# Token sums spread over the projection's last blocks, later statistics, and the first gates whole ahead of w_a

## The chip, the core and the metric

The kernel runs on one core of a Trainium2 chip. Its time is the device time of one execution in microseconds (us); lower is better. Five engines work side by side, each through its own queue in order: TensorE (PE) multiplies, VectorE (DVE), ScalarE (ACT) and GpSimd (POOL) do elementwise work, and SyncE (SP) issues most DMA transfers. An instruction at the head of a queue that waits for another engine holds up all that stands behind it in that queue.

## The reference, cut to what matters

One layer of a hybrid decoder, 1024 tokens and 16 meta tokens, width 1024, all in float32. Three branches are mixed through sigmoid gates, projected back, and followed by a SwiGLU MLP.

```python
xn = rms_norm(h, norm1_g)
p = xn @ w_in
(u_pool, q, c_lat, q_idx, k_idx, w_idx, cb, cc, cu, g_raw) = split_columns(p)
y_a = pool_mixer(u_pool, pool_w, pool_scale) @ w_a
attn = dsa_attention(q, q_idx, w_idx, rms_norm(c_lat, kv_norm_g), k_idx)   # top-k selection, then attention
y_b = attn @ w_b
y_c = short_conv_mixer(cb, cc, cu, conv_w) @ w_c
g = sigmoid(g_raw + b_gate).reshape(B, L, 3, 1024)
m = g[:, :, 0] * y_a + g[:, :, 1] * y_b + g[:, :, 2] * y_c
h = h + m @ w_o
hn = rms_norm(h, norm2_g)
gate, up = split(hn @ w_gate_up, 2)
h = h + (silu(gate) * up) @ w_down
return rms_norm(h, final_g)[:, 16:]
```

## The kernel before, in words

**Arithmetic.** A float32 factor is held as a high part (`whi`, `xh`, a cast on ACT) and a low part (`wlo`, `xl`, a subtraction on DVE or POOL, L288 in `sub_lo`). A product of two factors is three matmuls: high by high (L261), high by low (L262), low by high (L263). Tokens stand in two chunks of 512 columns, and outputs in tiles of 128 rows, so nearly every matmul is 128x128 by 512 columns. A large projection is cut into two by two blocks and computed with seven products instead of eight. For that, sums of the token blocks ("token sums", the keys T1 to T4) and sums of the weight blocks (the `sw` tiles, on POOL) are made first, and each is split into high and low parts before PE can use it. A product has four blocks of 128 along its inner dimension, so 12 matmuls; `CHAINED` is the order of the seven products of a job or of an MLP tile `f`. Four of the seven end in a result that is read from a PSUM bank as `c` by an ACT copy and later added to (DVE) as the other products come.

**Order.** The order of the work is written out by hand. `gemm` issues the matmuls and calls at its k-th step what a table `at` hangs there. `later` holds what consumes the product before it. `ahead` and `make_ahead` issue the making of weight factors a fixed number of products before PE needs them. `settle` issues low parts that were put off in `behind`. Since the queues run in order, a step that is called earlier in the program stands earlier in every queue that it uses. The indexer's top-k search (L726, L771, L772 on DVE, L790 to L796 on ACT) fills gaps from a background list, at a pace set by `pace_until`.

**The gates** (`gates`, `plan_gates`, from L1000). The first of these jobs is a plain product with two weights ("in" units). Before w_a, each weight is multiplied with chunk 1 only; after w_a, the same two weights come again (the "again" units, loaded and split a second time) and are multiplied with chunk 0, 24 matmuls each. Then come the chained products n=0, 1, 2 and so on, whose factors are made `n + 5` ahead. The token sum T4 of the input (L1253, three DVE operations for each of four blocks, then a cast L1268 and a low part) is spread by `PLAIN` and `SCHED` over these products.

**The output projection** (`out_proj`) runs blocks (o, ch) for output tile o and chunk ch. Blocks 0 to 4 take both chunks in turn, then 5, 6, 7 take chunk 0, then chunk 1. A block ends in an add of the residual (L1706, DVE), a scaling (L1696), a square (L1715, ACT) and an accumulation (L1719, POOL). Between its matmuls the token sums of the MLP are made: `first` (L1740, splits of the scaled tokens), `t1`, `t2`, `t3`. The norm's statistics are small matmuls (L1648) of the accumulated squares: `stat(0)` for chunk 0, `stat1` for chunk 1; `ratio` (L1663) spreads a statistic over the partitions.

**The MLP** (`mlp`) begins with f=0. The table `entry` hangs what is left of the token sums and statistics on its products. `pair_sums` (L1862 to L1865) are the four POOL sums of the weights of a tile f; they wait for its weights to be loaded (`raw`). For w_down, blocks of its weights are loaded by `load_w` (L2007) at slots counted from its first product, activations come back by `load_x` (L2014), and `split_x` (L2022) splits them.

Of the kernel before, what the change touches and what calls it, by code (L numbers as in the profile page):

```python
# [16 lines left out]
P = 128  # L17
# [37 lines left out]
SCHED = {0: (("T4b", 0), ("T4", 1)), 1: (("T4b", 1), ("T4", 2)), 2: (("T4b", 2), ("T4", 3)), 3: (("T4b", 3),),  # L55
         4: (("lo", 0),)}
# [22 lines left out]
def unit_plan():  # L79
# [22 lines left out]
    units.append(("again", cols[0], KT))  # L102
    units.append(("again", cols[0] + 4 * P, KT))
# [17 lines left out]
class Trunk:  # L121
    SLACK = 1500.0

    def __init__(self, tc, a):
# [806 lines left out]
    def branch_a(self):  # L931
# [72 lines left out]
        for j in range(2):  # L1004
            w = wg if j == 0 else self.get()
            xs = self.xn_real(1)
            if j == 0:
                pool_split(0)
                pool_product(1)
            ps = self.gemm(w, xs, 512)  # L1010
            if j:
                pool_product(0)
            t = self.t(self.xp, [P, 512], tag="b")
            self.gate(kind, o + 4 * j, t, ps)
            nc.sync.dma_start(self.sgd[kind, o + 4 * j, 1], t)
# [23 lines left out]
    def plan_gates(self):  # L1039
# [6 lines left out]
        n_op = 0  # L1046
# [12 lines left out]
        def plan(j):  # L1059
# [12 lines left out]

            def make(i):
                if not src:
                    start()
                factor(src[i], LO[i])
                if i == 0:
                    total(2, src["u", 0], src["u", 1], ALU.add)
                    total(4, src[2], src[0], ALU.subtract)
# [21 lines left out]
    def gates(self):  # L1101
# [70 lines left out]
        w = [self.get(), self.get(ahead=False)]  # L1172
        self.lo_engine = "pool"
        self.plan_gates()
        for a in range(2):
            self.make_ahead(PA[a])
            for name, k in PLAIN[a]:
                T[name](k)
            ps = self.gemm(w[a], self.xn_real(0), 512)
            self.later.append(lambda ps=ps, a=a: res(0, a, 0, copied(ps)))  # L1180
            flush_stores()
# [7 lines left out]
        for n, (j, i) in enumerate(self.order):  # L1189
            self.make_ahead(n + 5)  # L1190
# [476 lines left out]
    def out_proj(self):  # L1667
# [6 lines left out]
        self.opp = self.pool("op", 1)  # L1674
        tp = self.otp = self.pool("ot", 1)
# [24 lines left out]
        def block(w, o, ch, at=None):  # L1700
# [9 lines left out]
            if o == 0:  # L1710
                acc[ch] = self.t(tp, [P, 512], tag=f"acc{ch}")
# [9 lines left out]
        def first_stat(ch):  # L1721
            first_st[ch] = self.row_rstd([acc[ch], last[ch]], tp, scale=1.0 / 512, tag="rsp")
# [39 lines left out]
        def c(f, *a):  # L1762
# [8 lines left out]
              (4, 0): {1: c(bcast, 0), 3: c(first_stat, 1), 5: c(first, 0), 7: c(first, 1)},  # L1771
              (4, 1): {0: c(bcast, 1), 1: c(first, 2), 3: c(first, 3), 5: c(t1, 0), 7: c(t1, 1)}}
# [566 lines left out]
```

## Time and profile before

| | |
|---|---|
| median of 3 runs | 1720.79 us (1720.04 to 1721.91) |
| the profiled execution | 1719.1 us, of which its span is 1717.3 us |
| granted TensorE clock, mean over the span | 0.990 |
| PE busy | 1660.8 us, 97% of the span, 8008 matmuls |
| DVE, ACT, POOL busy | 74%, 45%, 42% |
| PE's share of the chain that ended last | 65% |

Every time below is counted from the start of the span. In a view of the timeline the columns are: start, length, engine, line, operation, output and input tiles, size, how many; and in brackets how long the engine was idle before it and what it waited for. A clock of 1.00 in a stretch is 2.4 GHz, 0.50 is 1.2 GHz.

### The profile page before, as it was taken

The numbers are of one execution on the slowest core, as the hardware profiler recorded it, in microseconds if no ns is written. First come the engines' busy times: TensorE is split into PE (matmuls) and PEld (weight loads), VectorE is DVE, ScalarE is ACT, GpSimd is POOL, SyncE is SP. The second block draws the span as 40 slices with busy tenths as digits, with TensorE's granted clock in tenths as the row PEclk, the third lists the DMA queues.
The fourth block names the chain that finished last, engine by engine and source line by source line (L and its number), as shares of the span: only waits on it lengthen the run. The fifth ranks groups of instructions, "written<-read, shape, count | busy, mean of one in ns | idle before, by whom it ended". The sixth has DMA issues, their size and how long they took to land.

```text
span 1717.3 us, 22774 instructions
## 1 busy us (share of the span) xinstructions
PE 1660.8 (97%) x8008; PEld 1383.6 (81%) x8008; DVE 1279.2 (74%) x2156; ACT 780.1 (45%) x1463; POOL 719.7 (42%) x537
## 2 busy tenths in 40 slices
PE   8989999998999999999999998999999999999998
PEld 7778878886888887888878876788888888778887
DVE  6999997578888853688787367666666666799787
ACT  5566227455544435776632233433333333444443
POOL 2412324415555766121075113555445554546043
PEclk9999999999999999999999998999999999999999
DMA  4111123132333343410077431323232333663433
GB/s 155 46 37 35 40 86 105 68 124 88 127 115 99 98 129 90 132 50 13 17 268 255 135 123 49 104 92 105 98 105 92 111 115 138 226 233 125 160 97 117
DMA packets 94227, 189.09 MB, mean 110 GB/s; under 512 B 9808, under 2 KB 23120, under 8 KB 94112
## 3 DMA queue, kind: packets, MB, share of 16 engines
q1 hardware_dynamic: 91008, 182.56, 31.7%
q10 hardware_dynamic: 2992, 4.75, 0.8%
q8 instruction: 63, 1.03, 0.3%
q0 software_dynamic: 112, 0.33, 0.1%
q14 instruction: 52, 0.43, 0.1%
HBM read 133.86 MB, written 53.74 MB: 109 GB/s over the span
## 4 chain that ended last, share of the span: by engine, by line
PE 65%; DVE 5%; DMA 2%; ACT 1%; issue 1%; SPq 0%; POOL 0%; ACTq 0%; DVEq 0%; POOLq 0%
PE ps L261 19%; PE ps L263 19%; PE ps L262 19%; PE ps L1452 2%; PE ps L1428 1%; PE ps L1429 1%; PE ps L1427 1%; PE ps L1476 1%; PE ps L1477 1%; PE ps L1478 1%; PE ps L1648 1%; DVE wlo L232 0%; DMA s<-ga 0%; DVE y L1696 0%; DVE B21l L288 0%
## 5 line engine op out<-in xcount | busy, mean ns | idle before, releaser
L261 PE MATMUL ps<-xh,whi 128*128 128x512 f32 (+1 forms) x492 | 174.2, 354 | 4.3 <-DVE u L869 2.4
L263 PE MATMUL ps<-xh,wlo 128*128 128x512 f32 (+1 forms) x492 | 173.6, 353 | 1.1 <-DVE wlo L232 1.1
L262 PE MATMUL ps<-xl,whi 128*128 128x512 f32 (+1 forms) x492 | 173.4, 352 | 0.6 <-POOL xl L288 0.4
L261 PE MATMUL ps<-h,whi 128*128 128x512 f32 x348 | 137.8, 396 | 3.8 <-ACT whi L226 2.4
L263 PE MATMUL ps<-h,wlo 128*128 128x512 f32 x352 | 138.3, 393 | 1.5 <-DVE wlo L232 1.5
L262 PE MATMUL ps<-l,whi 128*128 128x512 f32 x288 | 113.5, 394 | 1.3 <-DVE l L288 1.2
L261 PEld LDWEIGHTS ps<-xh,whi 128*128 128x128 f32 x492 | 93.1, 189 | 17.4 <-DVE u L869 2.8
L263 PEld LDWEIGHTS ps<-xh,wlo 128*128 128x128 f32 x492 | 93.2, 189 | 14.8 <-DVE wlo L232 1.9
L262 PEld LDWEIGHTS ps<-xl,whi 128*128 128x128 f32 x492 | 93.2, 190 | 13.3 <-POOL xl L288 1.2
L1862 POOL TENSOR_TENSOR l<-raw 128x512 f32<-128x512 f32 x21 | 30.8, 1468 | 153.9 <-DMA raw<-in_wts_dram 142.7
L232 POOL TENSOR_TENSOR wlo<-raw,whi 128x1024 fp32r<-128x1024 f32 x21 | 51.7, 2462 | 99.5 <-ACT whi L226 99.5
L726 DVE TENSOR_SCALAR_CACHE_REDUCE B<-sc,s 128x912 bf16<-128x912 f32 (+2 forms) x93 | 89.0, 958 | 0.1
L1917 ACT ACTIVATE c<-c 128x512 f32<-128x512 f32 x44 | 27.8, 632 | 125.4 <-DVE c L1954 125.4
L261 PEld LDWEIGHTS ps<-h,whi 128*128 128x128 f32 x348 | 65.7, 189 | 18.7 <-ACT whi L226 3.3
L263 PEld LDWEIGHTS ps<-h,wlo 128*128 128x128 f32 x352 | 66.5, 189 | 16.7 <-DVE wlo L232 2.4
L1954 DVE TENSOR_TENSOR c<-c,r 128x512 f32<-128x512 f32 x88 | 60.5, 688 | 17.6 <-ACT c L1917 15.4
L1913 ACT COPY c<-ps 128x512 f32<-128x512 f32 x66 | 38.7, 587 | 66.5 <-PE ps L263 63.8
L262 PEld LDWEIGHTS ps<-l,whi 128*128 128x128 f32 x288 | 54.5, 189 | 14.7 <-DVE l L288 2.8
L1908 DVE TENSOR_TENSOR c<-ps,c 128x512 f32<-128x512 f32 x66 | 45.3, 687 | 27.2 <-PE ps L263 27.1
L2026 POOL TENSOR_TENSOR raw<-raw,h 128x512 f32<-128x512 f32 (+1 forms) x12 | 18.6, 1547 | 102.6 <-DVE whi L288 48.6
L288 DVE TENSOR_TENSOR op<-raw,op 128x512 fp32r<-128x512 f32 (+1 forms) x43 | 34.3, 798 | 34.8 <-ACT op L1803 17.8
L1138 ACT COPY c<-ps 128x512 f32<-128x512 f32 x52 | 30.4, 585 | 63.9 <-PE ps L263 63.9
(556 smaller groups left out, 5465.3 us busy)
## 6 DMA issues: line engine op xcount, KB each, us to landing
raw<-in_wts_dram SPq DMA_DIRECT2D x120, 512.0 KB, 3.3
B<-y SPq DMA_DIRECT2D x33, 256.0 KB, 2.0
y<-b SPq DMA_DIRECT2D x32, 256.0 KB, 2.2
s<-y SPq DMA_DIRECT2D x32, 256.0 KB, 4.9
h<-in_wts_dram SPq DMA_DIRECT2D x24, 256.0 KB, 5.3
T<-h SPq DMA_DIRECT2D x22, 256.0 KB, 2.1
T<-y SPq DMA_DIRECT2D x22, 256.0 KB, 2.0
ga<-c SPq DMA_DIRECT2D x16, 256.0 KB, 3.6
```

What stands on the lines that cost most here:

```text
L232: e.tensor_tensor(l[:, c], r[:, c], h[:, c].bitcast(F32), op=ALU.subtract)
L261: nc.tensor.matmul(ps[:, c0:c0 + n], wh, xh, start=(start and k == 0), stop=False, **kw)
L262: nc.tensor.matmul(ps[:, c0:c0 + n], wh, xl, start=False, stop=False, **kw)
L263: nc.tensor.matmul(ps[:, c0:c0 + n], wl, xh, start=False, stop=(stop and k == last), **kw)
L288: getattr(self.nc, eng).tensor_tensor(lo, x, hi.bitcast(F32), op=ALU.subtract)
L726: nc.vector.tensor_scalar(junk2[:, :nk_of(i)], self.sc[i], value, None, op0=ALU.is_ge, op1=ALU.add, accum_out=at(cs, i))
L1138: nc.scalar.copy(t, ps)
L1452: nc.tensor.transpose(p3[:rows, h, :], d["S"][h][:, col:col + rows], self.ident)
L1862: e.tensor_tensor(s1, u[:, :512], u[:, 512:], op=ALU.add)
L1908: nc.vector.tensor_tensor(t, ps, t, op=ALU.add)
L1913: nc.scalar.copy(t, ps)
L1954: nc.vector.tensor_tensor(t, x, R[r], op=ALU.mult)
```

## The change

Three places are rewritten.

*The first gates.* The two plain weights are multiplied with both chunks ahead of w_a, and the "again" units are gone. w_a is followed at once by the chained products. Their factors 0 and 1 are made in w_a's last group, the first weight sums on POOL only after it, and `LEAD` makes factors 3 and more products ahead only as PE goes on (3 at n=0, 7 at n=3). The four blocks of T4 are hung on n=1, 2 and 3.

*The end of the output projection and the MLP's entry.* The steps `first`, `t1`, `t2`, `t3` move to later blocks, `stat(0)` from block (5, 1) to (6, 1), `ratio(0)` from block (6, 1) to the MLP's product n=1, `stat1` from n=0 to n=2, `ratio(1)` from n=1 to n=3. Squares and sums of chunk 1 lie in a new pool that is released after n=2. The four low and high parts of T4 are settled at n=4 instead of n=3.

*The start of w_down.* The first blocks "11" of w_down go to the homes of the `sw` tiles instead of the two `raw` buffers, and loads stand at other slots. The c tiles of the MLP get 6 buffers instead of 8.

```diff
-SCHED = {0: (("T4b", 0), ("T4", 1)), 1: (("T4b", 1), ("T4", 2)), ...
+SCHED = {1: (("T4", 0), ("T4", 1)), 2: (("T4b", 0), ("T4", 2)), ...
+LEAD = {0: 3, 1: 4, 2: 5, 3: 7}
...
-    units.append(("again", cols[0], KT))
-    units.append(("again", cols[0] + 4 * P, KT))
...
             w = wg if j == 0 else self.get()
-            xs = self.xn_real(1)
-            ...
-            ps = self.gemm(w, xs, 512)
+            for ch in (1, 0):
+                ...
+                ps = self.gemm(w, self.xn_real(ch), 512)
+                ...
+                self.gate(kind, o + 4 * j, t, ps)
...
         for op in range(4):
             self.act_on = 0 < op < 3
-            w = self.get()
+            w = self.get(ahead=op < 3)
+            if op == 3:
+                self.lo_engine = "pool"
+                self.plan_gates()
             for j in range(2):
                 for ch in range(2):
+                    if op == 3:
+                        self.make_ahead(2 if j and ch else j)
...
+            def first_sums():
+                total(2, src["u", 0], src["u", 1], ALU.add)
+                total(4, src[2], src[0], ALU.subtract)
...
-        w = [self.get(), self.get(ahead=False)]
-        self.lo_engine = "pool"
-        self.plan_gates()
-        for a in range(2):
-            self.make_ahead(PA[a])
-            ...
-            ps = self.gemm(w[a], self.xn_real(0), 512)
-            ...
+        self.first_sums()
...
-            self.make_ahead(n + 5)
+            self.make_ahead(LEAD.get(n, n + 5))
...
-                sq = self.t(tp, [P, 512], tag="sq", bufs=2)
+                sq = self.t(self.o2p, [P, 512], tag="sq", bufs=2)
...
-        block(w5, 5, 1, {1: c(first, 7), 3: c(stat, 0), 4: c(t2, 0), 6: c(t3, 0)})
+        block(w5, 5, 1, {1: c(first, 6), 2: c(self.ahead, 1), 4: c(t1, 3), 6: c(first, 7)})
...
-        return self.t(cs, [P, 512], tag="c", bufs=8)
+        return self.t(cs, [P, 512], tag="c", bufs=6)
...
-                if o % 2 == 0:
-                    pair = self.t(self.wp, [P, 1024], tag="raw", bufs=2)
-                    W[g, "11", o], W[g, "11", o + 1] = pair[:, :n], pair[:, 512:512 + n]
-                t = W[g, "11", o]
+                pool, tag = self.home("sw", (1, 0, 3, 2)[o])
+                t = W[g, "11", o] = self.t(pool, [P, 512], tag=tag)[:, :n]
...
-            when(-7 + o // 2, load_w, 0, "11", o)
+            when(-7 + 2 * (o // 2), load_w, 0, "11", o)
...
-        entry = {0: {0: lambda: [self.t2(3), self.settle()], 3: stat1},
-                 1: {1: lambda: self.ratio(1), ...
-                 ... 2: {0: each(t4, 0, 1), 2: lambda: [each(t4, 2, 3)(), self.settle()]}}
+        entry = {0: {0: lambda: [self.t2(3), self.settle()], 2: lambda: self.t3(2)},
+                 ...
+                 4: {0: stat1, 1: each(b22, 0, 1), 3: each(b22, 2, 3)},
+                 2: {0: lambda: self.ratio(1), 1: each(t4, 0, 1)},
+                 5: {0: lambda: [each(t4, 2, 3)(), self.settle()]}}
+        hold = {0: 3, 1: 4}
...
-                ahead(n_done - 1 + AHEAD)
+                ahead(hold.get(n_done - 1, n_done - 1 + AHEAD))
...
-                if cs is None:
-                    ahead(6)
+                if n_done == 1:
                     self.otp.release()
                     cs = self.pool("cs", 1, side="right")
+                if n_done == 3:
+                    ahead(6)
+                    self.o2p.release()
```

The first place, ACT's queue where w_a ends and the chained products begin. Before, the first chained weight sums (`whi`, `wlo` from `sw`), the copies of the two plain products and two T4 casts:

```order
L1053 CAST whi_3885<-sw_3850 128x512
L1053 CAST wlo_3888<-sw_3848 128x512
L1138 COPY c_3906<-ps_3857 128x512
L1230 ACTIVATE c_3906<-c_3906,cols_115 128x512
L1053 CAST whi_3930<-sw_3855 128x512
L1268 CAST T4h_772_3933<-c_3895 128x512
L1138 COPY c_3947<-ps_3899 128x512
L1230 ACTIVATE c_3947<-c_3947,cols_115 128x512
L1053 CAST wlo_3957<-sw_3891 128x512
L1268 CAST T4h_778_3960<-c_3936 128x512
L1138 COPY c_3975<-ps_3940 128x512
```

And now, from the cast of the first weight sum on; `ps_3904` is the bank that n=0, 2, 4 and 6 use in turn:

```order
L1054 CAST whi_3899<-sw_3897 128x512
L1054 CAST wlo_3917<-sw_3895 128x512
L1152 COPY c_3939<-ps_3904 128x512
L1054 CAST op_3947<-sw_3902 128x512
L1273 CAST T4h_771_3950<-c_3924 128x512
L1054 CAST op_3973<-sw_3920 128x512
L1054 CAST whi_3976<-raw_3689 128x512
L1273 CAST T4h_777_3981<-c_3928 128x512
L1235 ACTIVATE c_3939<-c_3939,cols_115 128x512
L1152 COPY c_3997<-ps_3904 128x512
```

Both copies of the bank now stand behind steps of the chained products: the first behind the two weight casts, the second behind two T4 casts and an activation of `c_3939`.

DVE's queue of the changed kernel from the low part of that first weight sum to the add whose result `c_3939` the activation reads:

```order
L284 TENSOR_TENSOR whi_3899<-sw_3897,whi_3899 128x512
L1258 TENSOR_TENSOR c_3924<-xh_5_84,s_3487 128x512
L1258 TENSOR_TENSOR c_3924<-c_3924,xl_21_100 128x512
L1258 TENSOR_TENSOR c_3924<-c_3924,s_3488 128x512
L1258 TENSOR_TENSOR c_3928<-xh_6_85,s_3489 128x512
L1258 TENSOR_TENSOR c_3928<-c_3928,xl_22_101 128x512
L1258 TENSOR_TENSOR c_3928<-c_3928,s_3490 128x512
L284 TENSOR_TENSOR op_3947<-sw_3902,op_3947 128x512
L1258 TENSOR_TENSOR c_3953<-xh_7_86,s_3491 128x512
L1258 TENSOR_TENSOR c_3953<-c_3953,xl_23_102 128x512
L1258 TENSOR_TENSOR c_3953<-c_3953,s_3492 128x512
L1147 TENSOR_TENSOR c_3939<-ps_3932,c_3939 128x512
```

Nine T4 operations and two low parts stand ahead of the add. In the kernel before, T4's first block stood beside the plain products and the first add of a chained product stood behind all twelve:

```order
L288 TENSOR_TENSOR T4l_773_3934<-c_3895,T4h_772_3933 128x512
L1253 TENSOR_TENSOR c_3964<-xh_7_86,s_3435 128x512
L1253 TENSOR_TENSOR c_3964<-c_3964,xl_23_102 128x512
L1253 TENSOR_TENSOR c_3964<-c_3964,s_3436 128x512
L288 TENSOR_TENSOR op_3984<-raw_3843,op_3984 128x512
L288 TENSOR_TENSOR T4l_779_3961<-c_3936,T4h_778_3960 128x512
L1253 TENSOR_TENSOR c_3993<-xh_8_87,s_3437 128x512
L1253 TENSOR_TENSOR c_3993<-c_3993,xl_24_103 128x512
L1253 TENSOR_TENSOR c_3993<-c_3993,s_3438 128x512
```

So the sums of T4 moved from beside the plain products to between the chained ones.

The second place, POOL's queue at the MLP's entry (f=0, before the weights of f=1 are used). Before, from the last accumulation of squares; `y` outputs of L288 are low parts of T4, `l` outputs of L1862 to L1865 the weight sums of f=1:

```order
L1719 TENSOR_TENSOR acc_1818_9261<-acc_1818_9261,sq_9896 128x512
L288 TENSOR_TENSOR l_2043_10114<-y_1920_9826,h_2040_10102 128x512
L288 TENSOR_TENSOR l_2050_10141<-y_1947_9943,h_2044_10116 128x512
L288 TENSOR_TENSOR y_2055_10157<-y_1893_9678,h_2051_10143 128x512
L288 TENSOR_TENSOR y_2058_10163<-y_1909_9762,h_2056_10159 128x512
L1862 TENSOR_TENSOR l_2060_10174<-raw_10136 128x512
L1863 TENSOR_TENSOR l_2061_10175<-l_2060_10174,raw_9872 128x512
L1864 TENSOR_TENSOR l_2062_10176<-raw_9872,l_2061_10175 128x512
L1865 TENSOR_TENSOR l_2063_10177<-raw_9872,raw_10136 128x512
```

And now:

```order
L1725 TENSOR_TENSOR acc_1812_9250<-acc_1812_9250,sq_9869 128x512
L284 TENSOR_TENSOR l_2036_10105<-y_1914_9798,h_2033_10089 128x512
L284 TENSOR_TENSOR l_2044_10134<-y_1937_9918,h_2037_10107 128x512
L1868 TENSOR_TENSOR l_2049_10154<-raw_10121 128x512
L1869 TENSOR_TENSOR l_2050_10155<-l_2049_10154,raw_9857 128x512
L1870 TENSOR_TENSOR l_2051_10156<-raw_9857,l_2050_10155 128x512
L1871 TENSOR_TENSOR l_2052_10157<-raw_9857,raw_10121 128x512
L284 TENSOR_TENSOR y_2054_10164<-y_1877_9639,h_2045_10136 128x512
L284 TENSOR_TENSOR y_2057_10170<-y_1898_9739,h_2055_10166 128x512
```

The two low parts of T4 changed places with the four weight sums of f=1.

The third place, SP's queue of transfers at the start of w_down. Before (x2 marks two transfers of one form in a row):

```order
L2007 DMA raw_13162<-in_wts_dram 128x512 x2
L2007 DMA raw_13183<-in_wts_dram 128x512 x2
L2014 DMA B11l_2523_13187<-B_1949_9949 128x512
L2014 DMA B11l_2525_13190<-B_1950_9950 128x512
L1925 DMA B_1959_9959<-y_2519_13172 128x512
L2014 DMA B11l_2530_13212<-B_1951_9951 128x512
L2014 DMA B11l_2532_13215<-B_1952_9952 128x512
```

And now:

```order
L2011 DMA l_2511_13152<-in_wts_dram 128x512
L2011 DMA l_2512_13154<-in_wts_dram 128x512
L2018 DMA B11l_2517_13175<-B_1939_9924 128x512
L2018 DMA B11l_2519_13178<-B_1940_9925 128x512
L1931 DMA B_1949_9934<-y_2514_13163 128x512
L2011 DMA l_2523_13199<-in_wts_dram 128x512
L2011 DMA l_2524_13201<-in_wts_dram 128x512
L2018 DMA B11l_2526_13204<-B_1941_9926 128x512
L2018 DMA B11l_2528_13207<-B_1942_9927 128x512
```

Two activations (`B11l`) are now asked for between the first and the second pair of weights, and the weights go to `l` tiles instead of `raw` buffers.

## Rows read from the trace of the kernel before

**Rows 1.** The page: the span, and busy time of each engine.

```profile
span 1717.3 us, 22774 instructions
PE 1660.8 (97%) x8008; PEld 1383.6 (81%) x8008; DVE 1279.2 (74%) x2156; ACT 780.1 (45%) x1463; POOL 719.7 (42%) x537
```

**Rows 2.** Timeline of PE: w_a's end, the waiting chained product, n=6 and the next.

```profile
386.81 0.39 PE L261 MATMUL ps<-xh,whi 128*128 128x512 f32 x1
...
410.46 0.79 PE L261 MATMUL ps<-s,whi 128*128 128x512 f32 x1 [5.59 <-ACT c L1138]
...
424.90 0.40 PE L261 MATMUL ps<-T4h,op 128*128 128x512 f32 x1
...
427.64 0.40 PE L261 MATMUL ps<-xh,op 128*128 128x512 f32 x1
```

**Rows 3.** Window: busy PE, PEld, DVE, ACT, POOL; PE's clock, DMA share, GB/s.

```profile
410.00:415.00 5.00, 4.54 (x11) 3.57 (x12) 4.90 (x7) 2.07 (x4) 1.70 (x1) 0.50 0.50 174
```

**Rows 4.** Timeline of ACT at the first gates.

```profile
390.62 1.07 ACT L921 COPY b<-ps 128x512 f32<-128x512 f32 x2
...
409.31 0.62 ACT L1268 CAST T4h<-c 128x512 fp32r<-128x512 f32 x1 [2.32 <-DVE c L1253]
409.83 0.58 ACT L1138 COPY c<-ps 128x512 f32<-128x512 f32 x1
```

**Rows 5.** Timeline of DVE at the first gates.

```profile
403.37 1.84 DVE L288 TENSOR_TENSOR whi<-sw,whi 128x512 fp32r<-128x512 f32 x1 [1.15 <-ACT whi L1053]
...
409.80 0.68 DVE L1253 TENSOR_TENSOR c<-xh,s 128x512 f32<-128x512 f32 x1
```

**Rows 6.** The page's DMA issues: count, size, median time to landing.

```profile
raw<-in_wts_dram SPq DMA_DIRECT2D x120, 512.0 KB, 3.3
...
y<-b SPq DMA_DIRECT2D x32, 256.0 KB, 2.2
```

**Rows 7.** Timeline of PE: start of block (5, 0), and of f=1.

```profile
1009.38 0.39 PE L261 MATMUL ps<-h,op 128*128 128x512 f32 x1
...
1084.93 0.39 PE L261 MATMUL ps<-B11h,wlo 128*128 128x512 f32 x1
```

**Rows 8.** PE's waits from 1000 to 1100: line, for what, us, times, longest.

```profile
PE ps L1648 <- ACT sq L1715: 4.8, 1, 4.8
PE ps L1648 <- POOL acc L1719: 2.8, 1, 2.8
PE ps L261 <- ACT whi L226: 2.4, 2, 2.0
PE ps L263 <- DVE wlo L232: 1.5, 2, 0.8
```

**Rows 9.** Timeline of DVE at the end of the projection.

```profile
1049.77 0.68 DVE L1706 TENSOR_TENSOR xt<-ps,xt 128x512 f32<-128x512 f32 x1
...
1060.22 0.68 DVE L1706 TENSOR_TENSOR xt<-ps,xt 128x512 f32<-128x512 f32 x1
```

**Rows 10.** Timeline of POOL from the projection's end to f=1.

```profile
1049.37 1.63 POOL L1864 TENSOR_TENSOR sw<-raw,sw 128x512 f32<-128x512 f32 x1
...
1076.01 3.16 POOL L288 TENSOR_TENSOR y<-y,h 128x512 fp32r<-128x512 f32 x2 [2.46 <-ACT h L1826]
1079.32 1.54 POOL L1862 TENSOR_TENSOR l<-raw 128x512 f32<-128x512 f32 x1 [0.15 <-DMA raw<-in_wts_dram]
...
1083.89 1.74 POOL L1865 TENSOR_TENSOR l<-raw,raw 128x512 f32<-128x512 f32 x1
```

**Rows 11.** PE's waits from 1470 to 1530, at the start of w_down.

```profile
PE ps L261 <- ACT c L1913: 2.1, 1, 2.1
PE ps L262 <- DVE B21l L288: 1.6, 1, 1.6
```

**Rows 12.** Timeline of SP's queue at the start of w_down.

```profile
1465.44 10.16 SPq L2007 DMA_DIRECT2D raw<-in_wts_dram  x4
```

**Rows 13.** Timeline of DVE at the start of w_down.

```profile
1481.10 0.70 DVE L288 TENSOR_TENSOR B11l<-B11l,B11h 128x512 fp32r<-128x512 f32 x1 [5.18 <-ACT B11h L2022]
```

More of the change, by code (lines that the diff above doesn't have):

```diff
@@ L1005, in branch_a @@
             w = wg if j == 0 else self.get()
-            xs = self.xn_real(1)
-            if j == 0:
-                pool_split(0)
-                pool_product(1)
-            ps = self.gemm(w, xs, 512)
[L1011 to L1015, printed above, removed]
+            for ch in (1, 0):
+                if j == 0 and ch:
+                    pool_split(0)
+                    pool_product(1)
+                ps = self.gemm(w, self.xn_real(ch), 512)
+                if j and ch:
+                    pool_product(0)
+                t = self.t(self.xp, [P, 512], tag="b")
+                self.gate(kind, o + 4 * j, t, ps)
+                nc.sync.dma_start(self.sgd[kind, o + 4 * j, ch], t)
         self.token_sums()
@@ L1075, in make @@
                     start()
-                factor(src[i], LO[i])
+                factor(src[i], LO[i] if j or i != 4 else "vector")
                 if i == 0:
-                    total(2, src["u", 0], src["u", 1], ALU.add)
-                    total(4, src[2], src[0], ALU.subtract)
+                    if j:
+                        first_sums()
+                    else:
+                        self.first_sums = first_sums
+                elif i == 1 and not j:
+                    self.first_sum5 = sum5
+                elif i == 4 and not j:
+                    self.first_sum5()
                 elif i == 1:
@@ L1721, in first_stat @@
         def first_stat(ch):
-            first_st[ch] = self.row_rstd([acc[ch], last[ch]], tp, scale=1.0 / 512, tag="rsp")
+            first_st[ch] = self.row_rstd([acc[ch], last[ch]], self.o2p, scale=1.0 / 512, tag="rsp")
             nc.gpsimd.tensor_tensor(acc[ch], acc[ch], last[ch], op=ALU.add)
@@ L1770, in out_proj @@
         at = {(3, 1): {4: c(first_stat, 0)},
-              (4, 0): {1: c(bcast, 0), 3: c(first_stat, 1), 5: c(first, 0), 7: c(first, 1)},
-              (4, 1): {0: c(bcast, 1), 1: c(first, 2), 3: c(first, 3), 5: c(t1, 0), 7: c(t1, 1)}}
+              (4, 0): {1: c(bcast, 0), 3: c(first_stat, 1)},
+              (4, 1): {0: c(bcast, 1), 1: c(first, 0), 4: c(first, 1)}}
         for o in range(5):
@@ L1777, in out_proj @@
         w5 = self.get()
-        block(w5, 5, 0, {2: c(t1, 2), 4: c(t1, 3), 6: c(first, 4)})
+        block(w5, 5, 0, {2: c(first, 2), 5: c(first, 3)})
         w6 = self.get()
-        block(w6, 6, 0, {3: c(first, 5)})
+        block(w6, 6, 0, {2: c(t1, 0), 6: c(first, 4)})
         w7 = self.get(ahead=False)
-        block(w7, 7, 0, {3: c(first, 6), 5: self.settle})
-        block(w5, 5, 1, {1: c(first, 7), 3: c(stat, 0), 4: c(t2, 0), 6: c(t3, 0)})
-        block(w6, 6, 1, {0: c(ratio, 0), 1: c(self.ahead, 1), 2: c(t2, 1), 4: c(self.ahead, 2), 5: c(t3, 1)})
-        block(w7, 7, 1, {1: c(t2, 2), 2: c(self.ahead, 3), 3: c(t3, 2), 5: c(self.ahead, 4), 6: self.settle})
+        block(w7, 7, 0, {1: c(t1, 1), 4: c(t1, 2), 6: c(first, 5)})
+        block(w5, 5, 1, {1: c(first, 6), 2: c(self.ahead, 1), 4: c(t1, 3), 6: c(first, 7)})
+        block(w6, 6, 1, {1: c(t2, 0), 4: c(t3, 0), 5: c(stat, 0), 6: c(self.ahead, 2)})
+        block(w7, 7, 1, {1: c(t2, 1), 2: c(self.ahead, 3), 5: c(t3, 1), 6: c(t2, 2), 7: self.settle})
     def operand(self, shape):
@@ L1856, in pair_sums @@
                 if j == 0:
-                    t = [self.t(self.otp, [P, 512], tag="sw", bufs=4) for _ in range(4)]
+                    t = [self.t(self.o2p, [P, 512], tag="sw", bufs=4) for _ in range(4)]
                 else:
@@ L2064, in mlp @@
             for k in range(len(GR[q // NK])):
-                when(-6 + k // 2 if q == 0 else -3 + k if q == 1 else 4 * (q - 2) + k, load_x, q, k)
+                when(-6 + k // 2 if q == 0 else -4 + k // 2 if q == 1 else 4 * (q - 2) + k, load_x, q, k)
         def run_events():
```

24 lines of the change are left out of this document (8 added, 16 removed).

## The prediction

> **What bounds the kernel now.** I read the busy times first: TensorE is busy 97% of the span, nothing else above 74% [rows 1]. So a change can only win or lose in the places where TensorE waits, or runs at the lower clock. No matmul of 512 columns is added or taken away here (the first two weights still meet both chunks, only at another time), so the sum is made of the waits at three places. I then read TensorE's waits and timeline there, and after them the queue that ended each wait.
>
> *The first gates.* From w_a's end at 386.81 to product n=6 at 424.90 [rows 2] are 38.1 us. They hold two plain products of 24 matmuls and six chained ones of 12, 120 in all. Twelve take 427.64 - 424.90 = 2.74 us [rows 2], so the work is 27.4 us and 10.7 us are lost. The largest wait is 5.59 us for an ACT copy [rows 2], which stood behind a T4 cast that itself waited for DVE [rows 4]. After it the clock was 0.50, the 1.2 GHz level, in all of 410 to 415 [rows 3], which costs another 2.5 us.
>
> *The projection's end and the MLP's entry.* From block (5, 0) at 1009.38 to the start of f=1 at 1084.93 [rows 7] are 75.6 us, for 228 matmuls, 52.1 us, and some small ones. 11.5 us go to four kinds of waits: 7.6 for the statistics of chunk 1 (the square, and POOL's accumulation), 3.9 for raw weights that were split late behind the token sums on DVE [rows 8].
>
> *The start of w_down.* 3.7 us of waits [rows 11]. SP held four weight transfers over 10.2 us [rows 12]; the activations behind them came late, and DVE stood idle 5.2 us [rows 13] before it had to work off a backlog.
>
> **The first gates, worked out.** Times are from w_a's end. Products n=0 and n=1 need only factors made ahead: 0 to 5.5. The next one, n=2, reuses the bank of n=0, whose ACT copy now stands behind two casts of the first weight sums. Those sums use memory that the last stores of w_a's results must have left. Before, the last two ACT copies of w_a ended at 391.69, 4.9 us after w_a [rows 4]. A cast and a low part of 1024 columns go from ahead of them; by twice the 0.62 and the 0.68 of 512 columns [rows 4, 5] that is at most 2.6 us; I take 2.3, so the copies end at 2.6. A store lands 2.2 us later [rows 6], at 4.8; one POOL sum of 1.63 [rows 10], two casts of 0.62 and a copy of 0.58 [rows 4] put n=2 at 8.2: 2.7 us lost.
>
> Product n=4 needs the next copy of that bank. On ACT it stands behind an activation, and that waits for a DVE add which stands behind eleven operations of 512 columns. DVE begins them at about 7.1. One of them takes 0.68 alone, and 1.84 beside POOL [rows 5], which at that time runs four operations of its own. An add that reads PSUM took 0.68 [rows 9] though POOL ran from 1049.37 to 1051.00 beside it [rows 10], so adds are not stretched. Eleven at 0.68 are 7.5 us; with three or four of them stretched by 1.16, 11 to 12.1 us; the add ends at 18.8 to 19.9, and with the activation and the copy n=4 starts at about 19.5 instead of 13.7. The wait of nearly 6 us is as long as the 5.59 of before, and I let it cost the same 2.5 us of lower clock. Products n=4 and n=5 then end at about 27.5; n=6 waits for another DVE add, some ten operations later, at about 28.5. Ideal would be 16.4: 12.1 us lost against 10.7, so **+1.4 us**. Bounds: with no DVE operation stretched n=4 starts at 16 and n=6 at 24.9, -2.2; with every one of the eleven stretched (12.8 us more, less what the late POOL leaves free) about +5.
>
> The Trainium skill, SBUF — State Buffer, section "Who interferes with whom", says that VectorE and GpSimd share one pair of ports as an exclusive lock, which concerns VectorE operations with two inputs in SBUF. The rows agree (0.68 with a PSUM input, 1.84 with two SBUF inputs). By that rule an operation waits for one POOL operation each, which is the three or four taken here; by a plain slowdown of all eleven it would be the upper bound.
>
> The second load and split of the two weights had its cover on engines that were not the bound: I give nothing for it beyond the 2.3 us above.
>
> **The projection's end, worked out.** With the token sums spread, the two splits of raw weights stand ahead of most of them on DVE, so I let blocks 5 to 7 run without a wait: TensorE reaches the MLP some 7 us sooner, at about 1044. But chunk 1's statistic needs the square of block (7, 1), whose add is the last of a DVE backlog. From the add of block (4, 1) at 1009.4 to that add are 56 operations: 47 of 512 columns at about 0.7, two of 1024, seven tiny ones, 36.5 us; nine or ten stretched by POOL's operations between add 10.5 us. The add ends at about 1056.8, against 1060.90 before [rows 9]. So the 7 us are mostly given back: TensorE idles from about 1050 to 1058, as it waited there before.
>
> From that add on the same queues count. Before, f=1's weights landed at 1079.32 [rows 10], and so were asked for at about 1075.9 by the 3.3 us of [rows 6], 15 us after the add. The changed kernel has four DVE operations more between, two of them tiny: 16.3 us, so asked for at 1073.1 and landed at 1076.5. Product n=4 starts 17 us after the add (25 DVE operations, and the casts between), and n=6 reaches its second block at about 1080.3. There it needs a low part of T4 from POOL. Before, that one was made at 1076.01 ahead of the four sums of f=1 [rows 10]. Now it stands behind them. The four took 1083.89 + 1.74 - 1079.32 = 6.3 us and a low part 1.6 [rows 10]: 1076.5 + 6.3 + 1.6 = 1084.4. TensorE waits 4.1 us; eight more matmuls, 1.8 us, and f=1 starts at 1086.2; with 1 us for a lower clock behind the wait, 1087.2 against 1084.93: **+2.3 us**. Bounds: if the sums don't bind, f=1 starts at 1082.1, -2.8; if the clock falls for a full 5 us, +4.
>
> The pools, released later, and six c tiles instead of eight: a c tile lives for two or three products, and its reader is an ACT or DVE step of one product later. I cost both at nothing; a c tile that comes late would hold an ACT copy, at 2.7 us for a product.
>
> **The start of w_down.** The first two weights no longer wait for a raw buffer that DVE still reads, and two activations are asked for before the second pair. DVE then begins some 4 us sooner, where it stood idle for 5.2 [rows 13]. I take the 2.1 and 1.6 us of [rows 11] and 0.2 of the smaller ones behind: **-3.9 us**. Bounds: -4.4 (all) and 0 (the `sw` homes are still read when the load is due).
>
> **Sum.** +1.4 + 2.3 - 3.9 = -0.2 us on the profiled execution's 1719.1, so 1718.9. The median of the runs is 1.7 us above that execution, so 1720.6.
>
> **The rivals.**
>
> *The four sums don't bind (faster).* If the load is asked for earlier, or DVE is stretched less, the low parts of T4 are there when n=6 comes. The entry then gives -2.8 instead of +2.3: -5.3 us, 1715.5. For it speaks that the 56 operations before the add carry the largest estimate of the working (10.5 us of stretch), and everything after the add moves with it; against it, that the load hangs on the same add, so that both move together and the order on POOL stays. If the gates reach their lower bound as well, 1712.
>
> *The clock falls after every new wait (slower).* I counted 2.5 us once at the gates and 1 us at the entry. If the wait before n=2, and the 4 us before the end of f=0, are each followed by a stretch at 0.50 as in [rows 3], 2.5 and 1.5 us come on top: 1724.6. It decides from two such stretches on. For it: the one wait of this size at the gates did that. Against: 2.7 us is half as long, and no row shows a fall after so short a wait.
>
> *The w_down load doesn't do what it says.* If the tiles it goes to are still being read, the gain is 0 and the time 1724.5. Against it: those tiles' last readers are factors of the last MLP tile, several products earlier.
>
> **How the numbers follow.** This kernel's runs can tell a difference above 0.2%, 3.4 us: faster is below 1717.4, slower above 1724.2. The forecast has 0.42, the first rival 0.36, the second 0.15 and the third 0.07. So faster 0.36, same 0.42, slower 0.22. The range reaches from the first rival with the gates at their lower bound, 1712, to a slower case with the gates above their middle, 1728; the forecast's own range is 1717.4 to 1724.2.
>
> **What would show it.** In the changed kernel's profile: a wait of TensorE for an ACT copy of about 2.7 us at n=2 and of nearly 6 us at n=4; no waits for raw weights in blocks 5 to 7; a wait of about 7 us for chunk 1's square; a wait of about 4 us for a low part on POOL in the last product of f=0; no wait above 1 us in w_down's first 20 products. Wrong would be the entry if POOL's low part came first, and the gates if n=4 started within 3 us of n=3's end.

## The result and the profile after

The changed kernel takes 1730.49 us in the median of four runs (1729.51 to 1731.73), the kernel before, timed with it, 1720.41 (1719.48 to 1721.91): ratio 1.0058, 95% interval 1.0045 to 1.0071. It is slower by 10.1 us, outside the range. The profiled execution shown here has a span of 1727.9 us, 10.6 more than that of [rows 1]:

```profile
span 1727.9 us, 22781 instructions
PE 1663.9 (96%) x8008; PEld 1386.8 (80%) x8008; DVE 1278.7 (74%) x2155; ACT 776.8 (45%) x1459; POOL 714.6 (41%) x536
```

PE does the same 8008 matmuls and is busy with them 3.1 us longer, at a mean granted clock of 0.986 instead of 0.990; DVE, ACT and POOL have a little less to do. So the 10 us are waits and lower clock at the places that the change touches. How late PE is against the kernel before, read at the same matmul in both timelines, says at which:

| place | PE late by (us) | added there |
|---|---|---|
| start of the chained products, w_a and the plain products done | -1.7 | |
| product n=7, 427.64 before [rows 2], 436.82 now | +9.2 | +10.9 |
| block (5, 0) of the output projection, 1009.38 before [rows 7] | +9.8 | +0.6 |
| start of f=1, 1084.93 before [rows 7], 1098.39 now | +13.5 | +3.7 |
| just ahead of w_down | +13.8 | +0.3 |
| behind w_down's first products | +10.4 to +10.7 | -3.1 to -3.4 |

The first line is -1.7 for two reasons: w_a and what stands ahead of it take 0.5 us less, and the plain products lost 1.2 us to small waits where they stood before. The prediction counted its term of the gates from w_a's end, with the 12.3 us that the plain products took there. Counted so, 10.9 - 1.2 = 9.7 us were added where +1.4 was forecast. The 0.6 and 0.3 us behind the gates and the entry were not looked into.

**The gates.** Four stretches of PE, starting with n=0, n=2, n=4 and n=6, and the first matmul of n=7:

```profile
397.41 0.39 PE L257 MATMUL ps<-xh,whi 128*128 128x512 f32 x1
...
407.81 0.80 PE L257 MATMUL ps<-s,whi 128*128 128x512 f32 x1 [4.41 <-ACT c L1152]
...
419.62 0.79 PE L257 MATMUL ps<-xh,op 128*128 128x512 f32 x1 [3.72 <-ACT c L1152]
...
431.62 0.80 PE L257 MATMUL ps<-T4h,whi 128*128 128x512 f32 x1 [4.64 <-DVE c L1147]
...
436.82 0.39 PE L257 MATMUL ps<-xh,wlo 128*128 128x512 f32 x1
```

One large wait of 5.59 us [rows 2] has become three, at the very products that the forecast named, and n=6 starts 34.2 us after n=0 where the working had 28.5. Behind each the clock was low; the windows of 5 us (columns as in [rows 3]: busy time of the engines, then the granted clock):

```profile
405.00:410.00 5.00, 2.19 (x5) 1.81 (x6) 3.19 (x3) 2.14 (x4) 4.91 (x4) 0.60 0.00 0
410.00:415.00 5.00, 5.00 (x17) 3.94 (x17) 4.90 (x5) 1.66 (x3) 2.01 (x2) 0.72 0.32 105
...
420.00:425.00 5.00, 5.00 (x17) 3.96 (x17) 4.93 (x7) 3.43 (x8) 1.96 (x2) 0.69 0.53 159
425.00:430.00 5.00, 1.98 (x9) 1.31 (x7) 4.96 (x7) 2.40 (x5) 4.92 (x4) 0.99 0.00 0
430.00:435.00 5.00, 3.38 (x8) 2.71 (x9) 4.93 (x12) 4.33 (x10) 2.98 (x3) 0.50 0.08 10
```

The third number of busy time is DVE's: 4.90 to 4.96 of every 5 us from 410 on, while PE does 3.38 or less in two of these windows. Between 407 and 431 DVE is the bound, though over the span it is busy 74% and PE 96%. Its busy share alone would not show that: before, too, it was 4.90 of 5 us from 410 to 415 [rows 3] and 4.93 from 420 to 425, since steps of the search fill its gaps. What shows it is what ended the waits, and run 4 below. What ACT and DVE did there, first ACT:

```profile
401.92 1.07 ACT L917 COPY b<-ps 128x512 f32<-128x512 f32 x2
406.13 0.62 ACT L1054 CAST whi<-sw 128x512 fp32r<-128x512 f32 x1 [3.14 <-POOL sw L1072]
...
407.17 0.58 ACT L1152 COPY c<-ps 128x512 f32<-128x512 f32 x1
...
418.37 0.72 ACT L1235 ACTIVATE c<-c,cols 128x512 f32<-128x512 f32 x1 [2.64 <-DVE c L1147]
419.00 0.56 ACT L1152 COPY c<-ps 128x512 f32<-128x512 f32 x1
```

and DVE:

```profile
400.06 0.69 DVE L284 TENSOR_TENSOR wlo<-raw,wlo 128x512 fp32r<-128x512 f32 x1 [0.17 <-ACT wlo L1054]
...
406.78 1.09 DVE L284 TENSOR_TENSOR whi<-sw,whi 128x512 fp32r<-128x512 f32 x1 [4.04 <-ACT whi L1054]
407.80 1.78 DVE L1258 TENSOR_TENSOR c<-xh,s 128x512 f32<-128x512 f32 x1
409.61 1.65 DVE L1258 TENSOR_TENSOR c<-c,xl 128x512 f32<-128x512 f32 x1
...
413.36 1.73 DVE L1258 TENSOR_TENSOR c<-c,s 128x512 f32<-128x512 f32 x1
...
417.66 0.68 DVE L1147 TENSOR_TENSOR c<-ps,c 128x512 f32<-128x512 f32 x1
...
427.53 3.43 DVE L284 TENSOR_TENSOR T4l<-c,T4h 128x512 fp32r<-128x512 f32 x2
430.88 0.68 DVE L1147 TENSOR_TENSOR c<-ps,c 128x512 f32<-128x512 f32 x1
```

Read them as one chain. w_a's last copies on ACT end at 402.99. The second weight sum on POOL begins at 404.84, and its cast on ACT at 406.13; the copy behind it frees n=2's bank. DVE has stood idle for 4.04 us and only at 406.78 gets the low part behind which T4's sums stand. From then on it has no gap: add at 417.66, activation, copy, n=4; then the four low parts of T4, T4's last sums and two steps of the search (2.6 us), and the add at 430.88 that n=6 waits for.

**The entry.** PE's waits from 1000 to 1110 (waiting line, for what: us in all, times, longest), where [rows 8] stood before:

```profile
PE ps L1653 <- ACT sq L1721: 5.5, 1, 5.5
PE ps L257 <- ACT c L1919: 5.4, 2, 2.8
PE ps L258 <- POOL y L284: 5.2, 1, 5.2
```

The waits for raw weights are gone, as forecast. The third is the low part of T4. On POOL it stands behind the four sums, which wait for their load; POOL's rows:

```profile
1087.88 1.29 POOL L1868 TENSOR_TENSOR l<-raw 128x512 f32<-128x512 f32 x1 [5.57 <-DMA raw<-in_wts_dram]
...
1091.83 1.72 POOL L1871 TENSOR_TENSOR l<-raw,raw 128x512 f32<-128x512 f32 x1
1093.50 2.50 POOL L284 TENSOR_TENSOR y<-y,h 128x512 fp32r<-128x512 f32 x2
```

SP had asked for that load at 1082.89, so it was there 5.0 us later. And PE, from the waiting matmul to the start of f=1:

```profile
1094.82 0.79 PE L258 MATMUL ps<-y,whi 128*128 128x512 f32 x1 [5.18 <-POOL y L284]
1095.41 0.63 PE L259 MATMUL ps<-h,whi 128*128 128x512 f32 x1
...
1098.39 0.63 PE L257 MATMUL ps<-B11h,wlo 128*128 128x512 f32 x1
```

Here a matmul takes 0.43 us to the next instead of 0.23: the lower level of the clock again.

**w_down.** SP's queue, which [rows 12] show as four transfers over 10.2 us, now has two, and then the activations:

```profile
1478.56 4.21 SPq L2011 DMA_DIRECT2D l<-in_wts_dram  x2
1482.86 0.86 SPq L2018 DMA_DIRECT2D B11l<-B  x2
```

and in place of PE's waits of [rows 11] there are four small ones from 1480 to 1540, of 0.6, 0.5, 0.4 and 0.2 us; the two largest:

```profile
PE ps L257 <- DVE y L2098: 0.6, 1, 0.6
PE ps L257 <- ACT T1h L2026: 0.5, 1, 0.5
```

### The profile page after: what moved, and what is told of

It reads as the page before. It is cut to its first block, busy times and chain, and to the rows that moved or that the text cites. A ratio compares the mean times of both kernels' runs of the same rounds, so it can differ in the third digit from the quotient of the medians.

```text
span 1727.9 us, 22781 instructions
## 1 busy us (share of the span) xinstructions
PE 1663.9 (96%) x8008; PEld 1386.8 (80%) x8008; DVE 1278.7 (74%) x2155; ACT 776.8 (45%) x1459; POOL 714.6 (41%) x536
## 4 chain that ended last, share of the span: by engine, by line
PE 76%; DVE 15%; issue 3%; ACT 2%; DMA 2%; POOL 1%; SPq 0%; ACTq 0%; DVEq 0%; POOLq 0%
PE ps L257 21%; PE ps L258 21%; PE ps L259 21%; PE ps L1457 2%; DVE B L722 2%; DVE u L886 1%; PE ps L1433 1%; PE ps L1434 1%; PE ps L1432 1%; PE ps L1481 1%; PE ps L1482 1%; PE ps L1483 1%; DVE x L449 1%; DVE sc L654 1%; DVE b L1258 1%
## 5 line engine op out<-in xcount | busy, mean ns | idle before, releaser
L1919 ACT COPY c<-ps 128x512 f32<-128x512 f32 x66 | 38.7, 587 | 73.2 <-PE ps L259 70.5
L284 DVE TENSOR_TENSOR whi<-l,whi 128x512 fp32r<-128x512 f32 (+1 forms) x45 | 46.6, 1036 | 23.2 <-ACT whi L1809 23.2
L284 DVE TENSOR_TENSOR wlo<-l,wlo 128x512 fp32r<-128x512 f32 (+1 forms) x45 | 49.2, 1093 | 16.4 <-ACT wlo L1809 15.5
L284 DVE TENSOR_TENSOR op<-l,op 128x512 fp32r<-128x512 f32 (+1 forms) x42 | 45.3, 1080 | 18.6 <-ACT op L1809 18.3
```

The lines of the kernel that those rows point to most:

```text
L284: getattr(self.nc, eng).tensor_tensor(lo, x, hi.bitcast(F32), op=ALU.subtract)
L1919: nc.scalar.copy(t, ps)
```

## The experiments

Theory: the gates cost nearly all of it, because the T4 sums on DVE lost the cover of the plain products; the entry costs some 4 us through POOL's order; w_down gains. Rivals: the entry carries the loss; or the gates cost because the first weight sums wait for w_a's stores, and the T4 sums are innocent.

Runs 1 to 4 were timed on one chip, runs 5 to 8 on a second, runs 9 and 10 on a third, each time with the kernel before beside them (1721.79, 1721.19 and 1720.42 us), but without the changed kernel. So "under the changed kernel" compares with the 1730.49 us above across chips; the ratio to the kernel before, with its 95% interval, is the firmer number.

**1. The gates undone.** `SCHED`, the "again" units, the factors and `first_sums` as before; the rest of the change kept.

```diff
-LEAD = {0: 3, 1: 4, 2: 5, 3: 7}
+    units.append(("again", cols[0], KT))
...
-                self.make_ahead(LEAD.get(n, n + 5))
+                self.make_ahead(n + 5)
```

> The first gates put back as they were; entry and w_down as changed. Theory (most of the loss is in the gates: TensorE's waits there grew from 10.7 to about 18 us): 1721, that is +4 us at the entry and -3.3 us at w_down against the kernel before. Rival (the three places act on each other, so the loss of the gates comes back elsewhere): 1725 or more.

1720.85 us against 1721.79 for the kernel before there, ratio 0.9988 (0.9968 to 1.0007): the loss is gone with the gates. PE's wait for the low part of T4 was only 2.09 us here, since the load came 3.5 us after SP had asked for it (1076.41):

```profile
1079.88 1.28 POOL L1863 TENSOR_TENSOR l<-raw 128x512 f32<-128x512 f32 x1 [4.04 <-DMA raw<-in_wts_dram]
```

**2. The gates alone.** The projection's steps, `entry`, the pools and `load_w` as before.

```diff
-        block(w5, 5, 1, {1: c(first, 6), 2: c(self.ahead, 1), 4: c(t1, 3), 6: c(first, 7)})
+        block(w5, 5, 1, {1: c(first, 7), 3: c(stat, 0), 4: c(t2, 0), 6: c(t3, 0)})
...
-            when(-7 + 2 * (o // 2), load_w, 0, "11", o)
+            when(-7 + o // 2, load_w, 0, "11", o)
```

> Only the first gates changed. Theory: 1729.5 to 1730.5, +9 to +10 us against before, with the three waits of the changed kernel at n=2, n=4 and n=6 and a clock of 0.5 to 0.7 behind each. Rival: under 1726.

1731.75 us, ratio 1.0049 (1.003 to 1.0068), with the same three waits, 4.39, 3.91 and 4.82 us. Together with the run before this settles the place. The gates alone cost 10.0 us by the medians; by the ratio it is 8.4, with an interval from 5.2 to 11.7.

**3. POOL's order at the entry.** The two low parts of T4 are settled in product n=3 again, ahead of the four sums of f=1.

```diff
-                 2: {0: lambda: self.ratio(1), 1: each(t4, 0, 1)},
-                 5: {0: lambda: [each(t4, 2, 3)(), self.settle()]}}
+                 2: {0: lambda: self.ratio(1), 1: each(t4, 0, 1),
+                     3: lambda: [each(t4, 2, 3)(), self.settle()]}}
```

> The changed kernel, with T4's last low parts at the MLP's entry settled in the product before, so that they stand ahead of the four weight sums of f=1 on POOL again. Theory (POOL's order costs the 5.2 us wait in the last product of f=0): -4 to -6 us against the changed kernel, 1725 to 1726, and no wait for a low part on POOL. Rival (the statistic is late and only moves the wait to another place): within 2 us of the changed kernel.

1724.69 us, ratio 1.0014 (0.9994 to 1.0035): 5.8 us under the changed kernel by the medians, 7.6 by the two ratios; run 7 gives the step on one chip. POOL makes the low parts while it would have waited for the load (asked for at 1084.47, there after 4.8 us), and PE's wait and the low clock behind it are gone:

```profile
1084.11 3.18 POOL L284 TENSOR_TENSOR y<-y,h 128x512 fp32r<-128x512 f32 x2 [0.22 <-ACT h L1832]
1089.26 1.30 POOL L1868 TENSOR_TENSOR l<-raw 128x512 f32<-128x512 f32 x1 [1.96 <-DMA raw<-in_wts_dram]
```

**4. T4's sums taken out of the gates.**

```diff
-SCHED = {1: (("T4", 0), ("T4", 1)), 2: (("T4b", 0), ("T4", 2)), ...
+SCHED = {}
...
+        X["T4"] = X["B11"]
```

> The changed kernel without the token sums T4 of the gates (the seventh product of every gate job then uses other tokens, so that part of the computation is left out). Theory (DVE has no cover for the 12 sums and their low parts once the plain products stand ahead of w_a; it is the bound from n=2 to n=6): the waits at n=4 and n=6 go, the one of 4.4 us at n=2 stays: -9 to -11 us against the changed kernel. Rival (all starts too late because the first weight sum waits for w_a's last stores): n=4 and n=6 still wait for 2 us or more each, -5 us or less.

1718.91 us, ratio 0.9981 (0.9951 to 1.0011), and a profiled span of 1716.8, 11.1 us under the changed kernel's. That is as much as the gates cost, or more. Of the three waits only the first is left, unchanged (a new one of 1.61 us stands at 442.13), and the clock is back from 415 on. PE's timeline and the windows of this kernel:

```profile
407.69 0.50 PE L256 MATMUL ps<-s,whi 128*128 128x512 f32 x1 [4.41 <-ACT c L1151]
```

```profile
410.00:415.00 5.00, 5.00 (x19) 3.99 (x19) 2.77 (x6) 3.40 (x7) 2.31 (x3) 0.80 0.46 148
415.00:420.00 5.00, 5.00 (x24) 4.10 (x23) 4.62 (x11) 2.55 (x7) 3.71 (x4) 1.00 0.36 116
```

DVE is busy 2.77 of 5 us where it was busy 4.90. So T4's work on DVE makes the second and third wait; the first has another cause. The run takes this work out altogether, and the kernel before was not run without it. There the wait of 5.59 us, with 2.5 us of low clock behind it, hung on a T4 cast too [rows 4], so it would gain as well. How much of the 10 us is due to T4's new place, and how much of the run's gain to work that was left out, is not told apart.

**5. The first weight sums no longer behind w_a's stores.** T4's eight tiles are laid out first in their pool, so that the memory of the first sums is not that of the last results.

```diff
+        for k in range(4):
+            self.X["T4"].append(tuple(self.t(gp, [P, 512], F32R, tag=f"T4{x}{k}") for x in "hl"))
```

> The changed kernel with the T4 tiles laid out first in their pool, so that the first weight sums and the T4 sums come to lie in memory that w_a's last results and their stores don't use; nothing else changes place. Theory (n=2 starts late because the second weight sum waits for the landing of a store of w_a, n=4 and n=6 because DVE is full): n=2 starts about 3 us sooner, and the waits at n=4 and n=6 stay; -3 to -4 us against the changed kernel. Rival (the store is not what holds it): within 1 us.

1728.24 us, ratio 1.0039 (1.0024 to 1.0055); that is 2.3 us under the changed kernel by the medians, 3.3 by the ratios. The wait before n=2 falls to 1.16 us, two new ones of 0.70 and 0.55 us stand in n=1, and the wait before n=4 grows by 2.0:

```profile
402.87 0.50 PE L257 MATMUL ps<-xh,wlo 128*128 128x512 f32 x1 [0.70 <-ACT wlo L1054]
404.15 0.50 PE L259 MATMUL ps<-xh,wlo 128*128 128x512 f32 x1 [0.55 <-DVE wlo L284]
...
407.90 0.50 PE L257 MATMUL ps<-s,whi 128*128 128x512 f32 x1 [1.16 <-ACT c L1154]
...
419.37 0.80 PE L257 MATMUL ps<-xh,op 128*128 128x512 f32 x1 [5.73 <-ACT c L1154]
...
431.38 0.79 PE L257 MATMUL ps<-T4h,whi 128*128 128x512 f32 x1 [3.90 <-DVE c L1149]
```

n=0 started at 399.22 in this execution, 1.8 us later than in the changed kernel. Counted from n=0, n=2 comes after 8.7 us instead of 10.4, 1.7 us sooner where the theory had 3, and n=6 after 32.2 instead of 34.2. The rest went to w_a's tail. POOL now makes sums from 398.87 on, beside w_a's last work on DVE; two operations there took 1.67 and 1.25 us instead of 0.69 each, and w_a's last copies on ACT, ahead of n=2's, ended 7.1 us after n=0 instead of 5.6. So the stores do hold the first wait, and taking this hold away is worth 2 us: PE gets to n=4 sooner and stands before the same DVE queue.

**6. T4's first two blocks earlier on DVE as well,** ahead of the factor of n=2, and no steps of the search on DVE before n=7; with the edit of run 5.

```diff
-SCHED = {1: (("T4", 0), ("T4", 1)), 2: (("T4b", 0), ("T4", 2)), ...
+SCHED = {2: (("T4b", 0), ("T4", 2)), ...
...
         self.first_sums()
+        for k in range(2):
+            T["T4"](k)
+        self.pace = [0.0, 1.0, 0.0]
...
+            if n == 7:
+                self.pace_until((LAT - 11) * step, 1.0)
```

> As the run before, and the first two T4 sums stand ahead of the first chained factor on DVE, and the top-k search takes no place on DVE before n=7. Theory of DVE's capacity: n=6 starts when DVE is through with 20 operations, about 20 us after its last work for w_a: some 8.5 us lost instead of 18, -8 to -10 us against the changed kernel, 1721 to 1722. Rival (the queue order of ACT decides): -4 us or less.

1722.21 us, ratio 1.001 (1.0 to 1.0021), 6.0 us under run 5 on the same chip. Two of the three waits are nearly gone; a new one of 5.3 us stands inside n=2:

```profile
405.78 0.50 PE L256 MATMUL ps<-s,whi 128*128 128x512 f32 x1 [1.16 <-ACT c L1153]
...
411.83 0.79 PE L258 MATMUL ps<-s,whi 128*128 128x512 f32 x1 [5.31 <-DVE whi L283]
...
425.65 0.50 PE L256 MATMUL ps<-T4h,whi 128*128 128x512 f32 x1 [1.42 <-DVE c L1148]
```

It waits for the low part of the first weight sum, n=2's factor, which now stands behind six T4 sums on DVE. In this order too PE waits once for some 5 us, as it did before the change [rows 2]. From n=0 (397.08) to n=6 are 28.6 us, 12.2 above the 16.4 of the bare work, where the theory had 8.5 lost. The run changes the place of T4's sums and that of the search at once, so their shares are not told apart.

**7. Runs 3 and 6 together.**

> As the run before, with POOL's order at the MLP's entry put right as well. If the places add up: -14 to -16 us against the changed kernel, 1714 to 1716, faster than the kernel before by 0.25% or more. If they don't: 1718 or more.

1716.43 us, ratio 0.9967 (0.9954 to 0.998). 5.8 us under run 6 on the same chip, the worth of POOL's order a second time.

**8. The gates of before, with the changed entry in POOL's better order and the changed w_down** (the edits of runs 1 and 3).

> The first gates as before, the entry as changed but with POOL's order put right, w_down as changed. By the sum of the places: +4.0 of the entry less the 2 us wait and about 1 us of clock, less 3.3 us of w_down: 1717.5 to 1719. If POOL's order is worth 5 us here too: 1715.

1715.57 us, ratio 0.9969 (0.9958 to 0.998): below both kernels, at the second of the two forecasts, and with the gates of before not to be told from run 7. The rewritten gates, at their best here, give nothing that these runs can tell.

**9. w_down alone,** on the kernel before.

```diff
+                pool, tag = self.home("sw", (1, 0, 3, 2)[o])
+                t = W[g, "11", o] = self.t(pool, [P, 512], tag=tag)[:, :n]
...
-            when(-7 + o // 2, load_w, 0, "11", o)
+            when(-7 + 2 * (o // 2), load_w, 0, "11", o)
...
-                when(-6 + k // 2 if q == 0 else -3 + k if q == 1 else 4 * (q - 2) + k, load_x, q, k)
+                when(-6 + k // 2 if q == 0 else -4 + k // 2 if q == 1 else 4 * (q - 2) + k, load_x, q, k)
```

> The kernel before with the w_down part of the change alone. Theory (the two raw buffers held the loads): the waits of 2.1 and 1.6 us go, -3 to -4 us, 1717 to 1718. Rival (w_down gains only together with the changed entry): within 1 us of before.

1716.67 us against 1720.42, ratio 0.9977 (0.9967 to 0.9987): -3.75 us. Waits of 0.4, 0.3 and 0.2 us are left at the start of w_down.

**10. The projection's end and the entry alone,** on the kernel before, with the new pools, the six c tiles and `entry` as in the change.

> The kernel before with the entry's part of the change alone, POOL's order as in the changed kernel. Theory: +1 to +4 us against before (the statistic of chunk 1 comes about 4.5 us sooner, the wait for a low part on POOL takes that back and more, by 2 to 5 us as the load of f=1 lands). Rival (the entry as such is a gain and loses only beside the changed gates): below before.

1725.36 us, ratio 1.003 (1.002 to 1.0039): +4.9 us. The load came 4.5 us after it was asked for (1074.34), PE waited 3.1 us, and the clock fell:

```profile
1085.79 0.80 PE L262 MATMUL ps<-y,whi 128*128 128x512 f32 x1 [3.10 <-POOL y L288]
1086.38 0.63 PE L263 MATMUL ps<-h,whi 128*128 128x512 f32 x1
```

The three parts alone give +10.0 (run 2), +4.9 (run 10) and -3.75 (run 9), +11.1 together, against +10.1 for the whole change. That is a sum within the noise: the interval of run 2 alone is 6.5 us wide.

## Why the prediction was wrong

**The gates (+1.4; 9.7 in the trace, 10.0 alone): the step that failed.** The places were right: n=2 behind the casts, n=4 behind T4's sums, n=6 behind an add on DVE. What failed are the times at which DVE reaches its work and the second of these adds, and the low clock behind the last wait, which the sum had at nothing. In us from n=0's start, or for the way named:

| step | forecast | measured |
|---|---|---|
| last copy of w_a on ACT ends | 2.6 | 5.6 |
| DVE begins the low part ahead of T4's sums | 7.1 | 9.4 |
| from there to the end of the first add | 11.7 to 12.8 | 11.6 |
| from that add to the end of n=6's add | 8.6 to 9.7 | 13.2 |
| n=6 starts | 28.5 | 34.2 |
| low clock behind n=6's start | 0 | 2.5 |

The first stretch of DVE came out as worked: of the eleven operations three were stretched to 1.65 to 1.78 us, and the first, the low part, to 1.09. (The add at 417.66, which reads PSUM, took 0.68, but POOL stood idle then, so this row does not test the claim that such adds are not stretched.) The Trainium skill, SBUF — State Buffer, "Who interferes with whom", has a VectorE operation with two SBUF inputs contend with a GpSimd instruction that reads SBUF, and the trace agrees: POOL began three operations beside T4's sums (407.34, 409.11 and 413.24), one for each stretched one. I used this for the first stretch and not for the second. There all four low parts of T4 stood beside POOL (two at 1.77 and 1.78, two in the 3.43 above), about 1.05 us each above 0.68, 4.3 us in all, and the stretch took 3.5 to 4.6 us more than forecast. Two steps of the search, 2.6 us, stand in it as well; the working counted "some ten operations" and does not say whether they were among them. The rest of the 5.7 us by which n=6 came late is w_a's tail, 3.0 us late at its last copy. The cast and the low part that I took away from ahead of the last copies were not what held them; ACT had idled 1.36 us for a DVE operation just before, and DVE's operations there ran stretched as well (1.71 at 395.94). What I did not add is what the change puts there: the factors of n=0 and n=1, with two casts and, at 400.06, a low part on DVE directly ahead of the operation that ACT waited for.

I also had the clock in the wrong place. The 2.5 us that I counted behind n=4 cost nothing, for n=6 waited for DVE and not for n=4's end; by my own times, 27.5 against 28.5, they already cost nothing in the sum. The stretch behind n=6 counts in full: 436.82 - 431.62 = 5.20 us for 2.74 of work. So the second rival was right that the clock falls after every new wait (three here, one at the entry). Its 2.5 us stood behind n=2, where n=4's wait for DVE swallows them; that the same 2.5 were lost behind n=6 is luck. Its 1724.6 was still 5.9 us short. (The first rival's 1715.5 is a slip: 1720.6 - 5.3 = 1715.3.)

Behind these sizes stands, as I read it, one cause. The change moves 11 us of PE's work to the front, and what DVE, ACT and POOL did beside it is left with nothing to lie beside. Before, the first block of T4's sums was made beside the second plain product, from 396.88 to 400.97, and the low part of n=2's weight sum (cast on ACT from 400.45) on POOL, 2.9 us after n=0 had started at 399.15; one row of DVE and one of POOL:

```profile
396.88 0.68 DVE L1253 TENSOR_TENSOR c<-xh,s 128x512 f32<-128x512 f32 x1
```

```profile
402.09 1.31 POOL L288 TENSOR_TENSOR whi<-sw,whi 128x512 fp32r<-128x512 f32 x1
```

Now the block stands between the chained products, and the low part begins 9.4 us after n=0. The change has also moved this low part from POOL to DVE (`factor(src[i], LO[i] if j or i != 4 else "vector")`), to the head of the queue that then binds. DVE idles 4.04 us before it with T4's sums behind it; in run 6 the sums that stand ahead of it begin at 403.88, and PE then waits 5.3 us for the low part. No run put it back on POOL by itself. The way from n=0 to n=6 grew from 25.8 us to 34.2. Run 4 shows that T4's work makes two of the three waits. That the lost cover, and not the new order or the moved low part, is what costs the 8.4 us is argued from the times and not shown. I costed the second load and split that went away, and not what the products had covered.

**The entry (+2.3; 3.7 in the trace, 4.9 alone): right mechanism, two sizes off.** On the scale of the kernel before (less 9.8 us) TensorE reached the MLP at 1043.9 (forecast 1044), the last add of the projection ended at 1056.3 (1056.8), the load was asked for at 1073.1 (1073.1), and PE stood before the low part at 1079.9 (1080.3). The load took 5.0 us instead of the median 3.3 of [rows 6], the four sums 5.7 instead of 6.3, and the last eight matmuls ran at the lower clock, 3.6 us instead of 2.8. f=1 started at 1088.6 on that scale; 1087.2 was forecast. The first rival, that the sums don't bind, fell with the wait that the trace shows; runs 3 and 7 give 5.8 us for the step, against the 5.1 between the forecast and that rival.

**w_down (-3.9; -3.1 to -3.4 in the trace, -3.75 alone): right,** with the waits of [rows 11] gone and small ones left. The third rival fell with it.

**Still open.** Why f=1's load was there 3.5 to 5.0 us after it was asked for. Its bytes moved in the same time: the last moved 2.9 us after the request in the changed kernel and in run 1 and 3.1 in the kernel before, while POOL began 5.0, 3.5 and 3.6 us after it. What held the end of that wait was not tried. Nor was it tried what holds w_a's tail on DVE, what n=2's low part costs there, or what the kernel before gains without T4.

## What to carry to other kernels

Work of the bounding engine that is moved forward can leave other engines' work without cover: list what the other engines did beside it, and ask what stands beside that now. Where one queue then becomes the bound for 25 us, sum that queue's operations with their stretched durations to the last wait, not to the first. And where a split on an engine in order can go ahead of work that waits for a load, it should: here the order of two low parts and four sums was worth 5.8 us (run 7 against run 6), more than the gain of the whole w_down edit.

## What was unexpected of the hardware

The clock fell to its lower level after shorter waits than the one of [rows 2]: after 4.41, 3.72, 4.64 and 5.18 us in the changed kernel, and after 3.10 in run 10, where the next matmuls stand 0.43 us apart. After a wait of 2.84 us (1071.88) they did too, but only eight small matmuls stood between it and the wait of 5.5 before; after one of 2.52 us (1082.99) they were 0.23 apart from the second on. And one 512 KB load was there 3.5 to 5.0 us after it was asked for, in kernels whose bytes took the same time.
